# A hybrid decoder layer on one core: value stores of one pass on GpSimd's queue, the leading tokens' values in two passes with 48 stationary columns, and another order of the query stores and loads behind them

## The chip, the cores and the metric

The kernel runs on one core of a Trainium2 chip. The metric is the device time of one execution in microseconds (us); less is better. The kernel before takes 1297.9 us, the median of three runs (1297.64 to 1297.99).

A core has five engines that run side by side, each through its own list of instructions in order: TensorE (PE, matmuls; its weight loads are shown as PEld), VectorE (DVE), ScalarE (ACT), GpSimd (POOL) and SyncE (SP). They wait for each other on semaphores. Transfers between the chip's memory and the core's are issued by SP or by POOL in the order of their lists, and are carried out by 16 DMA engines.

## The reference

One layer: 16 learned leading ("meta") tokens are put before 1,024 tokens of 1,024 features. The normed input goes through one projection, whose columns feed two groups of heads. Four heads follow a gated delta rule (a triangular system per chunk of 64 tokens, then a scan over the chunks), eight heads of 64 columns make softmax attention with a cumulative forget gate in the logits. Their outputs are joined and projected, a SwiGLU feed-forward layer follows, then a last norm. The leading tokens are dropped at the end. All in float32.

```python
h = jnp.concatenate([meta, x], axis=1)
u = rmsnorm(h, attn_norm_w[l])
proj = u @ w_in[l]
gq, gk, gv, gz, gb, ga, fq, fk, fv, ff = jnp.split(proj, IN_SPLITS, axis=-1)
o_gdn = gated_deltanet_group(jnp.concatenate([gq, gk, gv], axis=-1), gz, gb, ga, ...)
o_fox = forgetting_attention_group(fq, fk, fv, ff, fgate_b[l])
h = h + jnp.concatenate([o_gdn, o_fox], axis=-1) @ w_out[l]
h = h + swiglu(rmsnorm(h, ffn_norm_w[l]), w_gate[l], w_up[l], w_down[l])
return rmsnorm(h, final_norm_w)[:, N_META:]
```

## The kernel before

Every matrix product is made of three matmuls, to come near float32: both operands are split into a high part (`uh`, `whi`) and a low part (`ul`, `wlo`), and high x high, low x high and high x low are added in PSUM (`mm3g`, line 214). The input `u` lies transposed in `uh` and `ul`, eight blocks of 128 features by 1,040 tokens, the 16 leading ones first. Tokens are handled in eight tiles of 128 (t = 0 to 7), and the leading tokens are a tile of their own, t = -1.

The program goes through these stages: the projections for the delta heads with their convolutions (up to about 190 us), the inversion of the triangular systems, the levels that join blocks of it and the scan over the chunks (up to about 420 us), attention with the first output projection between (up to about 590 us), the feed-forward layer, and the last norm.

During inversion, levels and scan, PE has little of its own to do there, so the attention's projections are woven in as filler. The generator `fox` makes them in this order: gates `z0`, values in two passes (`fv1`, 264 columns with the forget gate's eight, then `fv0`, 256 columns; `b` is 1, then 0), keys (`fk`) and queries (`fq`). The object `od` keeps account of how long each engine is busy, and takes from the filler whenever the steps of the levels and the scan are not yet due; `LV0` is the account at which the two runs of levels become due. The order that it finds is written into PE's list.

Per value tile, `proj_tmg` makes 24 matmuls (three for each of eight blocks) with the tokens as the stationary operand. ACT copies the high part from PSUM into `fvt`, DVE subtracts for the low part, and SP stores to `v_d`, or to `vz_d` for the leading tokens (four copies, one for each quarter that `vm` reads). The tiles run from t = -1 to t = 7. `ps_mm` rotates through three PSUM banks, and `fvt` has a few buffers in rotation.

The queries run in 12 groups, four blocks `m` of 128 rows by three stretches of tokens (from 16, 358 and 700). Each is 24 matmuls of 340 or 342 columns into a bank of `ps_mm`, then a copy by ACT and a subtraction by DVE into `fhl` (lines 777 and 778), which has two buffers in rotation, and a store to `q_d` (line 780), issued by POOL. Keys go the same way to `k_d`.

Attention takes the heads one after another. `att_tiles` sets up tiles for one head parity, with memsets of rows of `ka` and `qa` on POOL (lines 727 and 728); `att_head` issues the head's loads on SP: `ka` and `qa` from `c_d`, then `kk`, `sa`, `ka`, `qa` from `k_d` and `q_d`, `avt` from `v_d`, and with head 1 also `vm`, both tiles of it. PE then makes scores (`sc`), transposes (`pt`) and outputs (`po`). Between them stand the matmuls of the delta heads' output projection, `wog`, whose results are added to a tile `ht` loaded from `x` and stored to `h_d`.

`tc.issue_after` puts an instruction behind another one of the same queue in that queue's list; it adds no wait.

Of the kernel before, what the change touches and what calls it, by code (L numbers as in the profile page):

```python
# [32 lines left out]
LV0 = (72.0, 106.0)  # L33
# [64 lines left out]
def tile_hymba_layer(ctx, tc, x, meta, attn_norm_w, w_in, conv_w, a_log, dt_bias, gdn_norm_w,  # L98
# [213 lines left out]
    for t in range(NT):  # L312
        load_norm(t)
        if w is None:
            w = win_block(GZ + 256, 264, "z1")
            nc.sync.dma_start(gnw, gdn_norm_w.rearrange("o p -> p o"))
        acc = proj_tm(t, w, 0, 264, f"z1_{t}")
        nc.vector.tensor_copy(gt[:, t], acc[:, 256:264])
        zst = gate_out(t, acc, zp, "zt", 2)
# [4 lines left out]
    load_norm(-1)  # L324
    acc = proj_tm(-1, w, 256, 8, "zg")
# [269 lines left out]

    def b3(col):
        return col[:, :, None].broadcast_to([col.shape[0], col.shape[1], P])
# [108 lines left out]
    def proj_tmg(acc, t, w, n):  # L706
        col, rows = tok_cols(t)
        yield from mm3g(acc[:rows, :n], [(uh[:, k, col:col + rows], ul[:, k, col:col + rows], w[0][k][:, :n],
                                          w[1][k][:, :n]) for k in range(KT)], n / 2400)
# [52 lines left out]
    def fox_proj(dst, chunks, off, scale, nm):  # L762
        for b in range(2):
            w = fox_w.pop(0)
            for i in range(2):
                m = 2 * b + i
                for ci, (c0, n) in enumerate(chunks):
# [12 lines left out]
                    last[0] = nc.gpsimd.dma_start(dst(m)[:, :, c0 - off:c0 - off + n], hl[:, :, :n].bitcast(F32))  # L780
# [148 lines left out]
    def fox():  # L929
# [8 lines left out]
        for b in (1, 0):  # L938
            n = 256 + 8 * b
            w = fox_w.pop(0)  # L940
            for t in range(-1, NT):
                if t == (3 if b else 1):
                    fox_load()
# [3 lines left out]
                vt = fvp.tile([P, 4, 2, DH], F32R, tag="fvt", name=f"fvt{b}_{t}")  # L947
                av = acc[:rows, :256].rearrange("p (h d) -> p h d", d=DH)
                split(vt[:rows, :, 0], vt[:rows, :, 1], av)
                src = vt[:rows].rearrange("p h a d -> p h (a d)").bitcast(F32)  # L950
                if t < 0:
                    for j in range(GRP):
                        vst[0] = nc.sync.dma_start(
                            vz_d[4 * b:4 * b + 4, VZ * j:VZ * j + NM * 512].rearrange(
                                "h (r f) -> r h f", f=512)[:, :, 0:P], src)
                else:
                    vst[0] = nc.sync.dma_start(v_d[4 * b:4 * b + 4, col:col + rows].rearrange("h t d -> t h d"), src)
# [32 lines left out]
    att_tiles(1)  # L990
    hds[1] = att_head(1)
    while od.step_fill():
        pass
    uctx.close()
# [184 lines left out]
    def wout_gdn(nb, tt):  # L1179
# [9 lines left out]
        with tc.issue_after(h_st[-2].ins) if len(h_st) >= 2 else nullcontext():  # L1189
            nc.gpsimd.dma_start(ht, x[cols, nbc])  # L1190
# [556 lines left out]
```

## Time and profile before

| what | value |
| --- | --- |
| median of 3 runs | 1297.9 us (1297.64 to 1297.99) |
| the profiled execution, its own time | 1296.32 us |
| its span in the trace | 1294.6 us |
| granted clock of PE, mean | 0.998 |
| PE busy | 1277.3 us, 99% of the span |
| DVE, ACT, POOL busy | 840.4, 546.3, 367.9 us |
| DMA | 234.90 MB, 181 GB/s in the mean |

A row of the timeline gives the start in us from the span's start, the duration, the engine, the line and operation, out<-in, sizes, how many, and in square brackets the idle time of the engine before it and what ended that. PE's matmuls overlap one another by the way they are shown: their pace is the distance from start to start. A row of the chain of waits gives start, duration, and what the end of the program was waiting for then. A row of the list of waits gives the waiting engine, tile and line, what it waited for, the total in us, how often, and the longest. A row of the windows gives a stretch, its length, busy time (and the count of instructions) of the engines asked for, PE's granted clock, the busy share of the DMA engines, and GB/s. SPq and POOLq are issues of transfers.

### The profile page before, as it was taken

The numbers are of one execution on the slowest core, as the hardware profiler recorded it, in microseconds if no ns is written. First come the engines' busy times: TensorE is split into PE (matmuls) and PEld (weight loads), VectorE is DVE, ScalarE is ACT, GpSimd is POOL, SyncE is SP. The second block draws the span as 40 slices with busy tenths as digits, with TensorE's granted clock in tenths as the row PEclk, the third lists the DMA queues.
The fourth block names the chain that finished last, engine by engine and source line by source line (L and its number), as shares of the span: only waits on it lengthen the run. The fifth ranks groups of instructions, "written<-read, shape, count | busy, mean of one in ns | idle before, by whom it ended". The sixth has DMA issues, their size and how long they took to land.

```text
span 1294.6 us, 19961 instructions
## 1 busy us (share of the span) xinstructions
PE 1277.3 (99%) x7434; PEld 1126.3 (87%) x7434; DVE 840.4 (65%) x1508; ACT 546.3 (42%) x940; POOL 367.9 (28%) x342
## 2 busy tenths in 40 slices
PE   8999999999999999999999999999999999999998
PEld 8999999999999888887778888888888888888887
DVE  6567899574267488886887666655656664465645
ACT  6455444133234477884453323333333343433332
POOL 2012213102333212213405534455433453020301
PEclk9999999999999999999999999999999999999999
DMA  6433634677498778838434654553445468945513
GB/s 231 133 114 116 178 93 105 171 199 225 151 338 260 200 217 222 226 79 269 163 130 153 196 165 147 179 187 130 147 155 170 156 212 290 375 179 201 208 63 130
DMA packets 181840, 234.90 MB, mean 181 GB/s; under 512 B 19160, under 2 KB 132080, under 8 KB 178928
## 3 DMA queue, kind: packets, MB, share of 16 engines
q1 hardware_dynamic: 176048, 215.74, 52.0%
q0 software_dynamic: 5696, 17.90, 4.2%
q8 instruction: 58, 0.95, 0.3%
q14 instruction: 38, 0.31, 0.1%
HBM read 154.68 MB, written 78.92 MB: 180 GB/s over the span
## 4 chain that ended last, share of the span: by engine, by line
PE 89%; DMA 4%; DVE 3%; issue 2%; ACT 1%; POOL 1%; SPq 1%; POOLq 0%; DVEq 0%; ACTq 0%
PE xp L1628 9%; PE yp L1628 7%; PE ua L1453 5%; PE ga L1453 5%; PE gb L1453 5%; PE ud L1453 5%; PE gd L1453 5%; PE ub L1453 5%; PE pj_fk L214 4%; PE fv L214 3%; PE pt L1071 2%; PE ue L1453 2%; PE ge L1453 2%; PE wog L214 2%; PE z L214 2%
## 5 line engine op out<-in xcount | busy, mean ns | idle before, releaser
L166 DVE TENSOR_TENSOR al_p<-ra_p,ah_p 128x2048 fp32r<-128x2048 f32 (+1 forms) x21 | 46.6, 2221 | 93.9 <-ACT ah_p L165 93.9
L165 ACT CAST ah_p<-ra_p 128x2048 fp32r<-128x2048 f32 (+1 forms) x21 | 37.1, 1766 | 106.0 <-PE xp L1628 48.5
L1628 PE MATMUL xp<-wh_p,al_p 128*128 128x512 f32 (+1 forms) x176 | 67.3, 382 | 0.0
L1628 PE MATMUL xp<-wl_p,ah_p 128*128 128x512 f32 (+1 forms) x176 | 67.3, 382 | 0.0
L1628 PE MATMUL xp<-wh_p,ah_p 128*128 128x512 f32 (+1 forms) x176 | 67.3, 382 | 0.0
L1509 POOL TENSOR_TENSOR gzw<-gzw,uzt 128x512 f32<-128x512 f32 x11 | 18.4, 1676 | 164.9 <-DVE uzt L1498 113.6
L1453 PE MATMUL gb<-uh_p,w_g_p 128*128 128x512 f32 x176 | 57.8, 389 | 0.0
L1453 PE MATMUL ub<-uh_p,w_u_p 128*128 128x512 f32 x176 | 57.8, 389 | 0.0
L1453 PE MATMUL gd<-uh_p,w_g_p 128*128 128x512 f32 x176 | 57.8, 389 | 0.0
L1453 PE MATMUL ud<-uh_p,w_u_p 128*128 128x512 f32 x176 | 57.8, 389 | 0.0
L1509 POOL TENSOR_TENSOR gxy<-gxy,uxy 128x512 f32<-128x512 f32 x22 | 38.3, 1740 | 66.5 <-DVE uxy L1498 58.7
L166 DVE TENSOR_TENSOR w_u_p<-raw_u,w_u_p 128x512 fp32r<-128x512 f32 x42 | 43.2, 1027 | 20.3 <-ACT w_u_p L165 20.1
L165 ACT CAST ph<-pt 128x512 fp32r<-128x512 f32 (+1 forms) x96 | 45.4, 477 | 23.4 <-PE pt L1071 20.6
L166 DVE TENSOR_TENSOR pl<-pt,ph 128x512 fp32r<-128x512 f32 (+1 forms) x96 | 51.9, 553 | 4.5 <-ACT ph L165 4.0
L1035 ACT ACTIVATE pr<-pr,sm 128x144 f32<-128x144 f32 (+3 forms) x64 | 50.6, 793 | 6.0 <-DVE sm L1030 5.7
L1453 PE MATMUL ua<-uh_p,w_u_p 128*128 128x512 f32 x160 | 52.5, 389 | 0.0
L1453 PE MATMUL ga<-uh_p,w_g_p 128*128 128x512 f32 x160 | 52.5, 389 | 0.0
L1628 PE MATMUL yp<-wh_p,ah_p 128*128 128x512 f32 x132 | 51.3, 389 | 0.0
L1628 PE MATMUL yp<-wl_p,ah_p 128*128 128x512 f32 x132 | 51.3, 389 | 0.0
L1628 PE MATMUL yp<-wh_p,al_p 128*128 128x512 f32 x132 | 51.3, 389 | 0.0
L165 ACT CAST w_u_p<-raw_u 128x512 fp32r<-128x512 f32 x42 | 26.0, 620 | 55.3 <-PE gd L1453 35.6
L166 DVE TENSOR_TENSOR wl_p<-rw_p,wh_p 128x2048 fp32r<-128x2048 f32 (+1 forms) x21 | 46.9, 2235 | 3.4 <-ACT wh_p L165 3.4
(651 smaller groups left out, 4250.0 us busy)
## 6 DMA issues: line engine op xcount, KB each, us to landing
ra_p<-ao_p SPq DMA_DIRECT2D x14, 1024.0 KB
raw_g<-in_w_gate_dram SPq DMA_DIRECT2D x22, 512.0 KB
raw_u<-in_w_up_dram SPq DMA_DIRECT2D x22, 512.0 KB
raw_d<-in_w_down_dram SPq DMA_DIRECT2D x22, 512.0 KB
wt_p<-raw_d SPq DMA_DIRECT2D x33, 256.0 KB
rw_p<-wt_p SPq DMA_DIRECT2D x8, 1024.0 KB
rw_p<-in_w_down_dram SPq DMA_DIRECT2D x6, 1024.0 KB
ao_p<-gzw SPq DMA_DIRECT2D x22, 256.0 KB
```

The costliest lines, as they stand in the source:

```text
L165: cast = nc.scalar.copy(dst_hi, src)
L166: low = nc.vector.tensor_sub(dst_lo, src, dst_hi.bitcast(F32))
L214: nc.tensor.matmul(dst, a, b, start=first, stop=last)
L1035: nc.scalar.activation(pr[:, :n], pr[:, :n], AF.Exp, bias=sm[:, np_ - 1:np_], scale=-1.0, accum_out=rsum[:, h, j:j + 1])
L1071: nc.tensor.transpose(pt[:, P * j:P * j + P], pts[j][0][:, j, c0:c0 + P], ident)
L1453: nc.tensor.matmul(dst, a[:, c], b[:, k], start=(first and k == 0 and i == 0), stop=(k == 3 and i == 2), skip_group_check=not first)
L1509: last_mul[0] = G.tensor_tensor(gs[d], gs[d], us[d], op=ALU.mult)
L1628: nc.tensor.matmul(dst[:, n_], a[:, f, c], b[:, f, n_], start=(first and i == 0 and n == 0), stop=(i == NF - 1 and n == 2), skip_group_che ...
```

## The change

It has seven parts.

1. **Leading tokens' values in two passes.** A new tile `um_` holds, for each block of 128 features, the 16 leading tokens' high part in columns 0 to 15, zeros, and their low part in columns 32 to 47. With it as the stationary operand, one matmul with `whi` and one with `wlo` make all products, 16 matmuls for 24. The rows 32 to 47 of the result (the low part's) are copied out by ACT into a new buffer `vlo`, and DVE adds the rows 0 to 15 to it; then the tile goes on as before. (The product low x low is now included.) `um_` is zeroed by POOL and filled by ACT and DVE.
2. **Order of the value tiles.** The leading tokens come fourth, behind tiles 0, 1 and 2.
3. **Value stores of the pass b = 0** (eight to `v_d`, four to `vz_d`) are issued by POOL instead of SP. What was to be issued behind the last value store on SP (`vst`) now stands behind that of the pass b = 1.
4. **Key weights** are asked for at t = 2 in the pass b = 0, the third tile as before. The load of `gnw` is issued behind those of the normed input.
5. **Query stores.** Once the scan has made its last output (`outs_left` is empty), they are issued by SP: the last four of twelve. The first two loads of `ht` go on SP as well.
6. **Head 1's tiles and loads** stand behind the last query store on SP.
7. `LV0` is lower by 2, as the filler is shorter.

```diff
-LV0 = (72.0, 106.0)
+LV0 = (70.0, 104.0)
...
+    um_ = lp.tile([P, KT, 48], F32R, name="um_")
+    nc.gpsimd.memset(um_.bitcast(F32), 0.0)
+    nc.scalar.copy(um_[:, :, 0:NM], uh[:, :, 0:NM].bitcast(F32))
+    nc.vector.tensor_copy(um_[:, :, 32:48], ul[:, :, 0:NM].bitcast(F32))
...
     def proj_tmg(acc, t, w, n):
         col, rows = tok_cols(t)
+        if t < 0:
+            for k in range(KT):
+                for i in range(2):
+                    nc.tensor.matmul(acc[:48, :n], um_[:, k], w[i][k][:, :n], start=not (k or i), stop=k + i == KT)
+                    od.pe(n / 2400)
+                    yield
+            return
...
-                    last[0] = nc.gpsimd.dma_start(dst(m)[:, :, c0 - off:c0 - off + n], hl[:, :, :n].bitcast(F32))
+                    last[0] = (nc.gpsimd if outs_left else nc.sync).dma_start(dst(m)[:, :, c0 - off:c0 - off + n], hl[:, :, :n].bitcast(F32))
...
-            for t in range(-1, NT):
-                if t == (3 if b else 1):
+            for t in (0, 1, 2, -1, *range(3, NT)):
+                if t == (3 if b else 2):
                     fox_load()
                 col, rows = tok_cols(t)
                 acc = (ps_mm if b or t % 2 else ps_t)(f"fv{b}_{t}")
                 yield from proj_tmg(acc, t, w, n)
                 vt = fvp.tile([P, 4, 2, DH], F32R, tag="fvt", name=f"fvt{b}_{t}")
+                if t < 0:
+                    lo = fvp.tile([P, 4, 2, DH], F32, tag="fvt", name=f"vlo{b}").rearrange("p a b c -> p (a b c)")[:NM]
+                    nc.scalar.copy(lo[:, :n], acc[32:48, :n])
+                    nc.vector.tensor_add(lo[:, :n], acc[:NM, :n], lo[:, :n])
+                    acc = lo
...
-                        vst[0] = nc.sync.dma_start(
+                        st_ = (nc.sync if b else nc.gpsimd).dma_start(
...
-                    vst[0] = nc.sync.dma_start(v_d[4 * b:4 * b + 4, col:col + rows].rearrange("h t d -> t h d"), src)
+                    st_ = (nc.sync if b else nc.gpsimd).dma_start(
+                        v_d[4 * b:4 * b + 4, col:col + rows].rearrange("h t d -> t h d"), src)
+                if b:
+                    vst[0] = st_
...
-    att_tiles(1)
-    hds[1] = att_head(1)
+    with tc.issue_after(last[0].ins):
+        att_tiles(1)
     while od.step_fill():
         pass
+    with tc.issue_after(last[0].ins):
+        hds[1] = att_head(1)
...
-        with tc.issue_after(h_st[-2].ins) if len(h_st) >= 2 else nullcontext():
-            nc.gpsimd.dma_start(ht, x[cols, nbc])
+        early = len(h_st) < 2
+        with tc.issue_after((ra_ld[NT - 1] if early else h_st[-2]).ins):
+            (nc.sync if early else nc.gpsimd).dma_start(ht, x[cols, nbc])
```

Three places show what this does to the lists. The first is POOL's list at the end of the query projection, before. The names `fhl_fq_358`, `_700` and `_16` are the query groups by their first token, `zmask` is a mask for the attention.

```order
L220 TENSOR_TENSOR os_4794<-os_4794,mhalf 128x4
L727 MEMSET ka_4869 6x1040
L728 MEMSET qa_4870 6x1024
L1190 DMA ht_0_5005<-in_x_dram 128x512
L1190 DMA ht_0_5041<-in_x_dram 128x512
L780 DMA q_d<-fhl_fq_358_4826 128x2x342
L780 DMA q_d<-fhl_fq_700_4889 128x2x340
L780 DMA q_d<-fhl_fq_16_4918 128x2x342
L1013 MEMSET zmask 128x1040
L780 DMA q_d<-fhl_fq_358_4947 128x2x342
L1014 AFFINE_SELECT zmask<-zmask 128x128
L780 DMA q_d<-fhl_fq_700_4976 128x2x340
```

The same place on POOL with the change:

```order
L220 TENSOR_TENSOR os_4786<-os_4786,mhalf 128x4
L792 DMA q_d<-fhl_fq_358_4820 128x2x342
L739 MEMSET ka_4861 6x1040
L740 MEMSET qa_4862 6x1024
L1035 MEMSET zmask 128x1040
L1036 AFFINE_SELECT zmask<-zmask 128x128
L1217 DMA h_d<-ht_0_4999 128x512
```

Of five query stores one is left, ahead of the memsets; four stores and both loads of `ht` are gone from this list.

The second place is SP's list with the change, from head 0's last load into head 1's (`ka_4861`, `kk_4958` and the others are head 1's).

```order
L767 DMA avt_4707<-v_d 128x8x128
L1213 DMA ht_0_4999<-in_x_dram 128x512
L1213 DMA ht_0_5035<-in_x_dram 128x512
L792 DMA q_d<-fhl_fq_700_4867 128x2x340
L792 DMA q_d<-fhl_fq_16_4896 128x2x342
L792 DMA q_d<-fhl_fq_358_4925 128x2x342
L792 DMA q_d<-fhl_fq_700_4954 128x2x340
L758 DMA ka_4861<-c_d 3x1040
L759 DMA qa_4862<-c_d 3x1024
L762 DMA kk_4958<-k_d 64x1040
L763 DMA sa_4959<-q_d 64x1024
L762 DMA kk_4958<-k_d 64x1040
```

Before, head 1's eleven loads followed head 0's `avt` directly. Now two loads of `ht` and four query stores stand between.

The third place is PE's list in the first pass over the values. Before, the leading tokens' matmuls came first, with 16 stationary columns (the first size in a row), three for each block:

```order
L214 MATMUL z_7_2692<-whi_z_1_2480,ul 128x256
L214 MATMUL fv_-1_2720<-whi_fv_0_2514,uh 16x264
L214 MATMUL fv_-1_2720<-wlo_fv_0_2515,uh 16x264
L214 MATMUL fv_-1_2720<-whi_fv_0_2514,ul 16x264
L214 MATMUL fv_-1_2720<-whi_fv_0_2514,uh 16x264
```

With the change they follow the third tile, two for each block:

```order
L214 MATMUL fv_2_2784<-whi_fv_1_2524,uh 128x264
L214 MATMUL fv_2_2784<-wlo_fv_1_2525,uh 128x264
L214 MATMUL fv_2_2784<-whi_fv_1_2524,ul 128x264
L716 MATMUL fv_-1_2814<-whi_fv_0_2518,um__2467 48x264
L716 MATMUL fv_-1_2814<-wlo_fv_0_2519,um__2467 48x264
```

Over the program PE's list is shorter by 16 matmuls.

More of the change, by code (lines that the diff above doesn't have):

```diff
@@ L315, in tile_hymba_layer @@
             w = win_block(GZ + 256, 264, "z1")
-            nc.sync.dma_start(gnw, gdn_norm_w.rearrange("o p -> p o"))
         acc = proj_tm(t, w, 0, 264, f"z1_{t}")
@@ L324, in tile_hymba_layer @@
     load_norm(-1)
+    nc.sync.dma_start(gnw, gdn_norm_w.rearrange("o p -> p o"))
     acc = proj_tm(-1, w, 256, 8, "zg")
```

## The prediction

> **What bounds the kernel now.** The first view is the page's head: busy time of each engine as a share of the span, and the chain that ended last.
>
> ```profile
> span 1294.6 us, 19961 instructions
> PE 1277.3 (99%) x7434; PEld 1126.3 (87%) x7434; DVE 840.4 (65%) x1508; ACT 546.3 (42%) x940; POOL 367.9 (28%) x342
> PE 89%; DMA 4%; DVE 3%; issue 2%; ACT 1%; POOL 1%; SPq 1%; POOLq 0%; DVEq 0%; ACTq 0%
> ```
>
> TensorE (PE) is busy for 99% of the span and makes 89% of the chain. So a change can gain in two ways only: fewer matmuls, or an end to one of the few places where PE stands still or runs slowly. The second view says how much there is of the latter: PE's own waits, longest first.
>
> ```profile
> PE wog L214 <- DVE fhl_fq L778: 1.9, 1, 1.9
> PE sc L1025 <- DVE sm L1030: 1.7, 3, 0.6
> ```
>
> The longest single wait is one of 1.9 us, by the first output projection (`wog`), for VectorE's (DVE's) eviction of a query tile. The third view is PE's timeline around it, the fourth the chain there, the fifth the granted clock in slices of 2 us.
>
> ```profile
> 433.27 0.31 PE L214 MATMUL pj_fq<-uh,wlo_fq 128*128 128x340 f32 x1
> 435.48 0.58 PE L214 MATMUL wog<-whi_wo,uh_p 128*128 128x512 f32 x1 [1.89 <-DVE fhl_fq L778]
> ...
> 439.23 0.40 PE L214 MATMUL wog<-whi_wo,uh_p 128*128 128x512 f32 x1
> ...
> 439.93 0.23 PE L1025 MATMUL sc<-ka,qa 70*128 70x144 f32 x1
> ```
>
> ```profile
> 413.01 6.61 DMA qa<-q_d
> 419.62 0.95 POOL ka L727
> 420.58 0.89 POOL qa L728
> 421.47 2.63 issue
> 424.09 0.59 POOL ht L1190
> ...
> 425.32 8.99 DMA q_d<-fhl_fq
> 434.42 0.47 ACT fhl_fq L777
> 434.91 0.53 DVE fhl_fq L778
> 435.48 4.61 PE wog L214 x12
> ```
>
> ```profile
> 434.00:436.00 2.00, 0.53 (x2) 0.94 1.08 255
> 436.00:438.00 2.00, 2.00 (x7) 0.50 0.71 241
> 438.00:440.00 2.00, 2.00 (x9) 0.71 0.50 190
> ```
>
> Read the chain from below. `wog` needs a PSUM bank; the bank is freed by an eviction into a buffer `fhl`; that buffer is freed when its earlier content has been stored to `q_d`; and that store was issued late, because on GpSimd (POOL) two memsets and two loads of `ht` stood ahead of it, and the first memset waited for head 0's `qa`. PE loses twice. Matmuls of 340 columns follow each other every 0.155 us, so the next was due at 433.43; it started at 435.48: **2.05 us**. Then the granted clock falls to half (0.50 in the second of the three slices), and nine `wog` matmuls take 439.23 - 435.48 = 3.75 us. The three behind them take 439.93 - 439.23 = 0.70 us, or 0.233 each; nine at that pace are 2.10: **1.65 us** lost.
>
> **The change part by part.** *Fewer matmuls.* The chain has the two passes over the 16 leading tokens and what follows them:
>
> ```profile
> 232.81 2.91 PE fv_-1_2720 L214 x24
> ...
> 241.72 17.83 PE fv L214 x144
> 259.56 2.76 PE fv_-1_3005 L214 x24
> ```
>
> 24 matmuls become 16 in each pass, with as many moving columns (264 and 256). At 2.91/24 = 0.121 and 2.76/24 = 0.115 us each, 8 x 0.121 + 8 x 0.115 = **1.89 us**. The stationary operand grows from 16 columns to 48:
>
> ```profile
> L214 PEld LDWEIGHTS fv_-1_2720<-whi_fv,uh x8: 93/94/98, 232.5 to 235.1; 128*16 128x16 f32 x8
> ```
>
> ```profile
> L214 PEld LDWEIGHTS fv<-whi_fv,uh x128: 186/188/193, 235.4 to 284.3; 128*128 128x128 f32 x128
> ```
>
> The full tiles, with loads of 188 ns, keep the same pace (17.83/144 = 0.124, a stall among them), so 48 columns, between the two, cost nothing.
>
> *Building `um_`.* A memset on POOL, a copy on ScalarE (ACT), one on DVE. DVE's stands ahead of the whole second inversion (`up`), and the eviction that PE waits for at 241.72 stands behind six `up` operations:
>
> ```profile
> 239.78 0.16 POOL L546 MEMSET ad<- 128x32 f32 x1 [10.59 <-DMA ad<-ad_d]
> ...
> 239.97 0.16 DVE L533 TENSOR_TENSOR up<-up,ad 128x2 f32<-128x2 f32 x1 [13.26 <-DMA rec_d<-zt]
> ...
> 241.02 0.40 DVE L166 TENSOR_TENSOR fvt_-1_2745<-fv_-1_2720,fvt_-1_2745 16x256 fp32r<-16x256 f32 x1
> ```
>
> DVE sits idle for 13.26 us before 239.97. The memset needs the store of `e`, which the sync queue issued before the load of `ad`:
>
> ```profile
> 232.03 0.53 SPq L516 DMA_DIRECT2D rec_d<-e  x1
> 232.78 2.57 SPq L545 DMA_DIRECT2D ad<-ad_d  x2
> ```
>
> If the store lands with the second `ad` load, a memset of 0.4 us (POOL takes 0.53 for 128x512 in this stage, by the next row) and a copy like the 0.16 rows push PE's stall at 241.72 out by 0.6 us; if it lands 0.6 us sooner, nothing.
>
> ```profile
> 228.32 0.53 POOL L547 MEMSET up<- 128x512 f32 x1 [3.22 <-DMA ud_d<-up]
> ```
>
> It is issued some 2 us ahead of that second load, so I take **0**, and keep 0.6 for the range. PE itself reaches that bank after 72 matmuls as before, since three full tiles now stand where the leading tokens and two tiles stood.
>
> *The second copy and add for the leading tokens (ACT, DVE), and the `fr` copy from `vlo`*: two operations of 0.4 us per pass, beside at least 2.8 us of matmuls per tile, with three banks rotating. Nothing. *Value stores of the second pass on POOL*: in PE's list of waits no value eviction stands but the one at 241.72, so there is nothing to gain. What it could cost: POOL's memset of `amt`, which comes after DVE's last `up`, now stands behind three of these stores, the third of them behind DVE's eviction of the third tile:
>
> ```profile
> 270.08 0.42 DVE L166 TENSOR_TENSOR fvt<-fv,fvt 128x256 fp32r<-128x256 f32 x1
> 270.42 0.68 DVE L535 TENSOR_REDUCE up<-up 128x16 f32<-128x512 f32 x1
> ```
>
> The eviction ends 0.6 us before `up` does, so the store's issue delays the memset by well under 1 us, in a chain of small DVE operations that runs on beside PE's value tiles. Nothing either way; the key weights keep their place, at the third tile.
>
> *Query stores.* `q_d` 358 of the third block now goes ahead of POOL's memsets, and the last four stores go on the sync queue (SP), behind two early loads of `ht` but ahead of all of head 1's loads. Each waits only for its own eviction. The wait of 1.89 us has then no cause left. The bank needed at 433.4 is that of the group that ends 2 x 3.8 us (24 x 0.157 each) earlier, so a store may be 6 us late before PE feels it. I take off **2.05 + 1.65 = 3.70 us**.
>
> *Head 1's loads.* This is the price. They went out from 419.65; now they stand behind the last query store. PE's last query matmul ends at 433.58, now 433.58 - 1.89 = 431.69; ACT 0.47 and DVE 0.53 make it 432.7, and the store and the two short `c_d` loads put the first `kk` at about 434.1. Head 0's loads show the rest, six of them (two `kk`, two `sa`, `ka`, `qa`, 1,544 KB):
>
> ```profile
> 409.91 0.50 SPq L750 DMA_DIRECT2D kk<-k_d  x1
> ...
> 413.01 0.59 SPq L753 DMA_DIRECT2D qa<-q_d  x1
> ...
> 419.65 0.46 SPq L750 DMA_DIRECT2D kk<-k_d  x1
> ```
>
> `qa` landed at 413.01 + 6.61 = 419.62, 9.7 us after the first issue. So head 1's `qa` lands near 443.8. Its first score stood at 451.26 and moves to 451.26 - 5.59 = 445.7: 1.9 us in hand. But `avt` (512 KB) and the first `vm` (256 KB) follow, and `vm` is read 0.5 us later:
>
> ```profile
> 451.26 0.32 PE L1025 MATMUL sc<-ka,qa 70*128 70x144 f32 x1
> ...
> 451.80 0.56 PE L1092 MATMUL po<-phm,vm 128*128 128x128 f32 x4
> ```
>
> 768 KB more take 4.8 us at head 0's 1,544/9.7 = 159 KB/us, or 3.0 us at the rate of the stretch in which these loads ran before:
>
> ```profile
> 420.00:440.00 20.00, 18.11 (x103) 16.88 (x101) 5.12 (x9) 4.63 (x9) 6.85 (x10) 0.91 0.97 257
> ```
>
> `vm` lands at 446.8 to 448.6 and is wanted at 446.2: PE waits 0.6 to 2.4 us. I take **1.0**, nearer to the second rate, which is that of the same loads. A part may be caught up in the attention, so nothing is not excluded.
>
> **The sum**, against the profiled execution: -1.89 - 3.70 + 1.0 = -4.6 us, a span of 1290.0 for 1294.6, and 1291.7 for its own 1296.32 us. That execution is 1.6 us below the median of 1297.9; with the same difference the median becomes **1293.3 us**.
>
> One rule of the Trainium skill is weighed here ("TensorE: Matmul & The Clock Gate", section "What's actually happening"): the clock goes back to half after an idle window of about 3.4 us, and the window runs free. The length of the half-clock stretch agrees (windows 434 to 440: 0.06 x 2 + 0.50 x 2 + 0.29 x 2 = 1.7 us of lost clock, 3.4 us at half), the cause does not, since PE stood still for only 2.05 us before it. Taken by the letter, no idle time under 3.4 us halves the clock; the sum would then have no reason to take off the 1.65.
>
> **The rivals.** *A: head 1's loads come late and the clock falls too.* For it: a pause of 1.89 us was followed by the half-clock stretch above; waits of 0.6 us (second row of PE's waits) were not, so the point lies between. At 2.4 us of wait and 1.65 more, the gain is 5.59 - 4.05 = 1.5 us: 1296.4. Against it: it needs the slow end of the rates. *B: the change does not do what it says, PE still waits at `wog`.* On the sync queue the stores share the DMA engines with head 0's last loads (busy share 0.97 in that stretch); should one take the 9 us that the chain shows for it, the wait stays and only the matmuls are gained: 1296.0. Against it: there are 6 us to spare, and head 1's loads are out of the way. *C: the slow clock is not tied to the pause* and 3.4 us of it turn up wherever PE pauses next: only 1.89 + 2.05 - 1.0 = 2.9 us are gained, 1295.0. The sentences on the skill above would have it so; the trace has one such stretch, right behind its longest pause, which speaks against. *D: slower.* All of head 1's loads stand in one queue behind a store. If that last store, issued at 432.7, holds the sync queue or the DMA engines for the chain's 8.99 us, `kk` to `qa` land at 441.7 + 9.7 = 451.4 and `vm` 3.0 to 4.8 later, 454.4 to 456.2: a wait of 8.2 to 10 us in two or three pieces and one half-clock stretch, 1.65. Net 5.59 - 9.9 = 4.3 us lost: 1302.2. It passes the time of before from a wait of 4 us (with the 1.65), and slower by 0.2% from 6.6. Against it: an issue on that queue costs the queue some 0.6 us (row at 413.01), not the whole transfer.
>
> **How the numbers follow.** Forecast 0.62; A 0.15; B 0.09; C 0.06; D 0.08. 0.2%, 2.6 us, is about what a measurement of this kernel can tell from no change. Faster than 1295.3 are the forecast, C and a small part of A (0.02): 0.70. Within are the rest of A and B: 0.22. Slower: D, 0.08. The range begins at 1291.5: no wait at all (5.59 gained, 1292.3) and 0.8 more, half of what PE's second row of waits could still give where the order shifts. It ends at 1297.0, which takes in A and B with the 0.6 of `um_`. Outside it lie D and some 0.1 from the ends.
>
> **What would show it.** In the profile after: 16 matmuls fewer; `fv_-1` groups of 8 with 48 columns, near 1.9 us a pass; PE's wait at `wog` for `fhl_fq` gone; a granted clock of 1.00 in all slices after the start; the stall in front of the fourth value tile still 0.3 us, not 0.9. Head 1's `kk` issued near 434; a new wait `sc<-ka,qa` or `po<-phm,vm` near 446, of 0 to 2.4 us. Wrong would make it: a second half-clock stretch there (A), `q_d` stores that take 9 us (B), or a new place in the passes of the values or the levels where PE waits.

## The result, and the profile after

| kernel | median | range, runs | ratio to before [95%] |
| --- | --- | --- | --- |
| before | 1297.95 us | 1297.64 to 1298.7, 4 | 1 |
| after | 1305.12 us | 1303.97 to 1308.28, 4 | 1.0057 [1.0042, 1.0071] |

The change makes the kernel 7.2 us (0.57%) slower, where 4.6 us less was predicted and the range ended at 1297.0. The profiled execution of after is the slowest of its four (1308.28 us, span 1306.6).

The page's head, in the order of the prediction: span, busy time, chain by engine.

```profile
span 1306.6 us, 19944 instructions
PE 1280.3 (98%) x7418; PEld 1129.2 (86%) x7418; DVE 839.8 (64%) x1511; ACT 547.9 (42%) x943; POOL 370.8 (28%) x349
PE 81%; DVE 6%; DMA 5%; issue 3%; SPq 2%; ACT 1%; POOL 1%; POOLq 0%; DVEq 0%; ACTq 0%
```

PE makes 16 matmuls fewer, as planned, but its share of the chain falls from 89% to 81%: it waits more. PE's own waits:

```profile
PE sc L1047 <- DMA qa<-c_d: 4.1, 1, 4.1
PE pu L645 <- ACT y L638: 3.1, 2, 2.9
PE po L1114 <- DMA vm<-vz_d: 3.1, 1, 3.1
```

The wait of `wog` is gone, and three longer ones have come: one in the levels (`pu`), two at the start of head 1's attention. The granted clock in slices of 2 us at both places (length, PE busy, clock, DMA share, GB/s):

```profile
292.00:294.00 2.00, 0.16 (x2) 1.00 1.05 377
294.00:296.00 2.00, 0.69 (x16) 0.57 0.85 279
296.00:298.00 2.00, 2.00 (x58) 0.50 0.12 37
...
454.00:456.00 2.00, 0.00 (x0) 0.67 1.10 293
456.00:458.00 2.00, 1.21 (x3) 0.50 1.09 282
```

At both places the clock falls to half while PE waits. Where the time goes can be read by setting the starts of the same matmuls in the two traces side by side:

| matmul | before, us | after, us | after minus before |
| --- | --- | --- | --- |
| last of the values (`fv`) | 284.65 | 283.46 | -1.19 |
| last of the queries (`pj_fq`) | 433.27 | 438.21 | +4.94 |
| 13th of `wog` | 440.40 | 441.59 | +1.19 |
| last `pt` | 580.11 | 591.34 | +11.23 |
| last of all | 1288.14 | 1299.73 | +11.60 |

So there are two gains, 1.2 us up to the last value and 3.75 us at `wog`, where 1.89 and 3.70 were predicted. And there are two losses: 6.1 us between the values and the last query, and 10.0 us at the start of the attention.

**The loss in the levels.** The chain of after there (start, duration, what was waited for):

```profile
286.98 2.30 issue
...
289.30 4.41 DMA v_d<-fvt
...
293.78 0.37 ACT fvt L165
294.15 0.36 ACT fhl_fk L789
294.52 0.45 ACT y L638
...
295.62 1.91 PE pu L645 x62
```

`pu` needs `y`, a copy by ACT. In ACT's list the copy stands behind a cast of values into `fvt`. That cast waits for a store of an earlier `fvt` to land, and the store itself was held back on GpSimd's queue.

**The loss in the attention.** The chain of after from the last query matmul to head 1's first output:

```profile
435.90 2.49 PE pj_fq L214 x16
...
438.41 0.73 ACT whi_wo L168
...
439.17 0.65 DVE wlo_wo L169
...
440.54 0.51 DVE fhl_fq L790
...
441.06 0.36 SPq L792
...
442.27 0.47 SPq L762
...
447.17 3.91 SPq L748
...
451.13 9.85 DMA vm<-vz_d
...
461.11 1.09 PE po L1114 x4
```

The last query's eviction stands behind casts of the weights `wo` on ACT and DVE. Then come its store, head 1's loads from 442.27 (`kk` is the first large one), and the loads of `vm`: the first takes 3.91 us to be issued on SP (L748), the next, issued at 451.13, takes 9.85 us to land.

### The profile page after: what moved, and what is told of

It is laid out like the page before. It is cut to its first block, busy times and chain, and to the rows that moved or that the text cites. A ratio compares the mean times of both kernels' runs of the same rounds, so it can differ in the third digit from the quotient of the medians.

```text
span 1306.6 us, 19944 instructions
## 1 busy us (share of the span) xinstructions
PE 1280.3 (98%) x7418; PEld 1129.2 (86%) x7418; DVE 839.8 (64%) x1511; ACT 547.9 (42%) x943; POOL 370.8 (28%) x349
## 4 chain that ended last, share of the span: by engine, by line
PE 81%; DVE 6%; DMA 5%; issue 3%; SPq 2%; ACT 1%; POOL 1%; POOLq 0%; DVEq 0%; ACTq 0%
PE xp L1651 9%; PE yp L1651 7%; PE gd L1476 4%; PE ua L1476 4%; PE ga L1476 4%; PE gb L1476 4%; PE ud L1476 4%; PE ub L1476 4%; PE pj_fq L214 3%; PE pj_fk L214 3%; PE pt L1093 2%; PE ue L1476 2%; PE ge L1476 2%; PE po L1118 1%; PE wog L214 1%
```

## The experiments

Each run was measured in a batch with before. Before's medians in these batches lie between 1297.2 and 1297.74 us, so the ratio is what compares. Each diff is against the kernel that is named ahead of it.

### The attention: parts 5 and 6

**e2_h1_early**, after with head 1's tiles and loads where they were:

```diff
-    with tc.issue_after(last[0].ins):
-        att_tiles(1)
+    att_tiles(1)
+    hds[1] = att_head(1)
...
-    with tc.issue_after(last[0].ins):
-        hds[1] = att_head(1)
```

> The changed kernel with another part undone: head 1's tiles and loads are no longer tied to the last query store, and go out behind head 0's again. Theory 1 (head 1's loads come too late and cost two waits, 4.1 and 3.1 us, and slow clock on top, some 9 us): both waits at 450 to 462 us go, the time falls to about 1296; the four query stores on SP now stand behind head 1's loads, so a wait of up to 2 us at wog may come back (then 1299). Rival (the loads are late because DMA is slower with the stores on SP, whatever their order): the waits stay above 2 us each, the time above 1302.

Measured: 1302.97 us, 1.0039 [1.0025, 1.0054]. The waits for `qa` and `vm` are gone, so part 6 makes them. But a wait of 1.0 us at `wog` is back, and one of 3.4 us (`sc` for DVE's `sm`) is new: the query stores on SP now stand behind head 1's loads.

**e7_q_part**, before with parts 5 and 6 alone (their lines of the change's diff, nothing else).

> The kernel before with the query part of the change alone: four query stores and two loads of ht on SP, head 1's tiles and loads behind the last of these stores. Theory (this part gains 3.7 us at wog and loses more to late loads of head 1, by itself): no wait at wog, slow clock there gone, then waits for qa and vm of head 1 of 3 us or more each with slow clock behind them; 1297.2 - 3.7 + 9 = 1302. Rival (head 1's loads are late only because the levels were late and moved other transfers): waits under 2.4 us in all, the time 1294 to 1296.

Measured: 1303.21 us, 1.0041 [1.0026, 1.0056]. The 13th `wog` starts 3.54 us earlier than before, so the predicted 3.70 is there. Then PE waits (the scores read `ka` and `qa`; the list names `avt` as the one that came last):

```profile
PE po L1094 <- DMA vm<-vz_d: 3.8, 1, 3.8
PE sc L1027 <- DMA avt<-v_d: 3.5, 1, 3.5
```

The chain of this run shows the two steps that the prediction mis-sized:

```profile
433.68 0.74 ACT whi_wo L168
...
435.81 0.51 DVE fhl_fq L778
...
437.55 0.47 SPq L750
...
444.89 11.31 DMA vm<-vz_d
...
456.34 1.09 PE po L1094 x4
```

The first `kk` goes out at 437.55. The last query matmul starts at 433.48 here, so that is 4.1 us later; the prediction had 434.1 - 431.4 = 2.7. And `vm` lands at 456.20, 18.7 us behind the first `kk`, where 9.7 + 3.0 to 4.8 were predicted.

**e9_vm_early**, as e7, with the loads of both `vm` right behind head 0's loads:

```diff
+        vm_load(i)
...
-        if h:
-            for i in (0, 1) if h == 1 else (h,):
-                vm_load(i)
+        if h > 1:
+            vm_load(h)
```

> e7_q_part with one thing moved: the four loads of vm (512 KB), which need no query, stand right behind head 0's loads instead of last in head 1's. Theory (a load's landing is set by all that is in the queue with it, not by what stands ahead of it: 512 KB less in the burst behind the last query store lets every other load land some 2 us sooner, and vm itself is there): no wait for vm (3.8 us in e7_q_part), the wait for ka, qa and avt falls from 3.5 us to 1 to 2 us, the time from 1303.2 to about 1297. Rival (loads land in the order of the queue, the 9.7 us of head 0's loads hold, and the wait comes from the late start alone): the wait for qa stays at 3.5 us and only that for vm goes, 1299 to 1300.

Measured: 1297.28 us, 0.9994 [0.9985, 1.0003], 5.8 us less than e7 when each is set against its own before. The two waits are one now:

```profile
PE sc L1027 <- issue: 2.8, 1, 2.8
```

Most of the 5.8 us is `vm`'s own: its wait of 3.8 us is gone, and the half clock behind the waits lasts 6.8 us instead of 10.2. But `vm` had not only been late itself. With its 512 KB out of the burst, the loads ahead of it come down 0.7 us sooner: the wait of 3.5 us in front of `sc` becomes one of 2.8, less than the fall to 1 to 2 us that was expected. ("issue" says that the profile shows nothing that ended it.)

**e8_repair**, before with the memsets of head 1 on DVE and the first two loads of `ht` on SP behind head 1's loads. The cause of the wait at `wog` goes, and head 1's loads stay early:

```diff
-        nc.gpsimd.memset(ka[:NA].bitcast(F32), 1.0)
-        nc.gpsimd.memset(qa[:NA].bitcast(F32), -1.0)
+        ms = nc.vector if i else nc.gpsimd
+        ms.memset(ka[:NA].bitcast(F32), 1.0)
+        ms.memset(qa[:NA].bitcast(F32), -1.0)
...
-        with tc.issue_after(h_st[-2].ins) if len(h_st) >= 2 else nullcontext():
-            nc.gpsimd.dma_start(ht, x[cols, nbc])
+        early = len(h_st) < 2
+        with tc.issue_after((h_ld[1] if early else h_st[-2]).ins):
+            (nc.sync if early else nc.gpsimd).dma_start(ht, x[cols, nbc])
```

> The kernel before with another way to free GpSimd's queue for the query stores: they stay on GpSimd, but the two memsets of head 1's tiles go to VectorE and the two first loads of ht to SP behind head 1's loads, which stay where they were. Theory (the wait at wog came from what stood ahead of the stores, and head 1's early loads are free): no wait at wog, no slow clock at 436 to 439 us, no wait for head 1; 1297.2 - 3.7 = 1293.5 us. Rival (the stores are slow because of head 1's loads on the DMA engines): the wait at wog stays above 1 us and the time above 1296.

Measured: 1294.44 us, 0.9981 [0.997, 0.9991]. In the median the wait at `wog` can be had away for 3.3 us, if head 1's loads are not made to pay for it. The profiled execution, 1296.56 us, does not keep the gain: its 13th `wog` starts 3.35 us before that of before, but its last `pt` 0.06 us behind. One of head 0's scores (`sc`) waits 2.1 us for `sm`, and 3.4 us of half clock come with it. `sm` stands in DVE's list behind the addition to `ht`, and the load of `ht`, now behind head 1's loads, lands only at 438.74.

### The value stores: part 3

**e1_vstores_sp**, after with the value stores of both passes on SP:

```diff
-                        st_ = (nc.sync if b else nc.gpsimd).dma_start(
+                        st_ = nc.sync.dma_start(
...
-                    st_ = (nc.sync if b else nc.gpsimd).dma_start(
+                    st_ = nc.sync.dma_start(
```

> The changed kernel with one part undone: the value stores of the second pass go back from GpSimd's queue to SP's. Theory 1 (the stores on GpSimd go one at a time: each is issued about 0.3 us after the one before has landed, so the fvt buffers come free late, ScalarE stands before a cast, and its copy of y comes late for TensorE): the wait of 2.9 us for y in the levels and the slow clock behind it go, the order offset of TensorE at 300 us falls from +4.8 to about -1.5 us, and the time from 1305.1 to about 1299. Rival (ScalarE and VectorE are late because of the sync queue, whose key weights and na loads changed places, or because of um_): the wait stays at 2 us or more and the time stays within 2 us of 1305.

Measured: 1308.72 us, 1.0093 [1.0077, 1.0108]: slower than after. The stall only moves: PE waits 2.5 us at `pj_fk` for the `fvt` of DVE.

**e3_both**, e1 and e2 together.

> Both parts undone at once: value stores on SP, head 1's loads ahead of the last query stores. What is left of the change: 16 matmuls fewer, the order of the value tiles, four query stores and two loads of ht on SP. If the two costs are all there is and add up, 1305.1 - 6 - 9 = 1290 us; with a wait at wog come back, 1294. If they overlap (the second starts only because the first shifts things), 1296 or more.

Measured: 1304.57 us, 1.0053 [1.0038, 1.0068]. It is no faster than e2: putting both parts back gains nothing over putting head 1's loads back alone.

**e4_halves**, after with each value store on GpSimd's queue made as two halves of two heads:

```diff
-                    st_ = (nc.sync if b else nc.gpsimd).dma_start(
-                        v_d[4 * b:4 * b + 4, col:col + rows].rearrange("h t d -> t h d"), src)
+                    for h0 in (0,) if b else (0, 2):
+                        hn = 4 if b else 2
+                        st_ = (nc.sync if b else nc.gpsimd).dma_start(
+                            v_d[4 * b + h0:4 * b + h0 + hn, col:col + rows].rearrange("h t d -> t h d"), src[:, h0:h0 + hn])
```

> The changed kernel with each value store of the second pass on GpSimd's queue cut into two of two heads each, 256 rows of 512 bytes instead of 512. Theory 1 (GpSimd's queue holds a limited count of rows in flight, at least 768 and under 1,024): the two halves of a store go out back to back, and the first half of the next one too, without waiting for a landing; only the fourth half waits. The wait for y shrinks or goes. Rival (each store waits for the landing of the one before, whatever its size): every half is issued about 0.3 us after the half before has landed, the eight stores take longer in all than before and the wait for y grows.

Measured: 1304.61 us, 1.0056 [1.0036, 1.0076], two runs, as after. Its profile loses 2.7 us in the levels where after's loses 6.1, but the median doesn't follow. GpSimd's list in after shows why halves were tried:

```profile
289.30 0.76 POOL L974 DMA_DIRECT2D v_d<-fvt  x1 [2.32 <-issue]
294.01 0.76 POOL L974 DMA_DIRECT2D v_d<-fvt  x1 [3.96 <-issue]
```

The store issued at 289.30 lands at 293.71 (chain above), and the next goes out 0.30 us after that: on this queue the stores go one at a time.

**e5_vst**, e1 with `vst` set by every store again (part 3 undone in full), and **e6_own_vlo**, e5 with `vlo` in a buffer of `fhl` instead of `fvt`:

```diff
-                if b:
-                    vst[0] = st_
+                vst[0] = st_
...
-                    lo = fvp.tile([P, 4, 2, DH], F32, tag="fvt", name=f"vlo{b}").rearrange("p a b c -> p (a b c)")[:NM]
+                    lo = fp.tile([P, 2, 348], F32, tag="fhl", name=f"vlo{b}").rearrange("p a c -> p (a c)")[:NM]
```

> The changed kernel with its third part fully undone: the value stores of the second pass on SP as in e1_vstores_sp, and the loads for the levels (ubk, na) again behind the latest value store instead of the last one of the first pass, so the second level's 1 MB of na leaves the stretch from 265 to 282 us. Theory A (that load crowds the value stores out, whose landings free the fvt buffers): the value stores land in 5 us or less, TensorE's order offset at the end of the levels falls from +4.2 us to 0 or below, the time from 1308.7 to 1304. Rival B (vlo takes one of only three fvt buffers, and the leading tokens' stores come fourth): the offset stays at +3 us or more and the time within 2 us of 1308.7.

> As e5_vst, and vlo in a buffer of the pool of fhl, which is unused then, instead of in the rotation of three fvt buffers. Rival B of e5_vst: the waits of ScalarE for v_d stores between 260 and 290 us shrink, TensorE's waits at the first key matmuls go, and the offset at the end of the levels reaches about -1.5 us; time 3 us or more below e5_vst. If theory A was all: no difference to e5_vst beyond 1 us.

Measured: 1307.38 us, 1.0082 [1.0062, 1.0102], and 1308.69 us, 1.0085 [1.0065, 1.0105]. Both have a wait of 2.5 us at `pu` for `y`, as after has. So neither GpSimd's queue nor the rotation of `fvt` makes the loss in the levels by itself: between the last value and the last query e5 still loses 4.4 us and e6 4.5, where after loses 6.1. Without part 3 the kernel is 9.6 us slower than before (e5), with it 7.2: part 3 saves some 2.5 us, if anything (the intervals overlap; that of e1 is clear of after's).

### The values and the levels: parts 1, 2, 4 and 7

**e10_um_mixed**, before with `um_` (`vlo` in `fhl`), part 7, and the leading tokens fourth in the pass b = 1, first in b = 0. **e11_um_fourth** has them fourth in both and the key weights at t = 2: parts 1, 2, 4 and 7, but with `vlo` in `fhl` and the load of `gnw` where it was. **e13_best** is e10 with the edit of e8. From e10 to e11:

```diff
-            for t in (0, 1, 2, -1, *range(3, NT)) if b else range(-1, NT):
-                if t == (3 if b else 1):
+            for t in (0, 1, 2, -1, *range(3, NT)):
+                if t == (3 if b else 2):
```

> The kernel before with the 48-column values alone (um_, 16 matmuls fewer, vlo in a buffer of the fhl pool, LV0 lower by 2), value stores and the loads behind them as before; the leading tokens fourth in the first pass but first in the second. Theory (the stall in the levels comes from the fourth place in the second pass, which puts the four stores of the leading tokens into SP's list ahead of the second block of key weights, whose cast stands ahead of y on ScalarE): no wait of TensorE for y above 0.5 us, its order offset against before at 350 us is -1.2 to -1.6 us, the time 1296. Rival (um_ and the order of the first pass delay VectorE's inversion by themselves): offset above 0 at 350 us, the time 1298 or more.

> As e10_um_mixed, but the leading tokens fourth in both passes, as the change has it, and the key weights asked for at t = 2. Theory: the second block of key weights lands about 2 us later than in e10_um_mixed, TensorE waits some 2.5 us for y, the clock falls, offset at 350 us +2 to +3 us, the time about 1301. Rival of e10_um_mixed: no difference between the two beyond 1 us.

> e8_repair (memsets on VectorE, early ht on SP behind head 1's loads, query stores on GpSimd) together with e10_um_mixed (48 columns, leading tokens first in the second pass). If the two gains add: 1294.4 - 1.4 = 1293. If the 48 columns bring no gain by themselves: 1294 to 1296.

Measured: 1299.79 us, 1.0014 [1.0005, 1.0024]; 1300.94 us, 1.0021 [1.0012, 1.0031]; 1297.54 us, 0.9998 [0.9989, 1.0007]. The 48-column part alone does not gain 1.89 us but loses 2.1 to 3.3, although the last value matmul of e11 starts 1.15 us earlier than before's. The place of the leading tokens, with the key weights, makes 1.2 us of it in the medians, and the intervals overlap. Two causes were left: the second pass's value weights come late behind the leading tokens' stores (W), or part 7 (L).

**e15_lv0**, before with part 7 alone. **e14_um_lv0**, e11 without part 7:

```diff
-LV0 = (70.0, 104.0)
+LV0 = (72.0, 106.0)
```

> The kernel before with part 7 alone: LV0 of 70 and 104. The loads na and ubk of the first level then stand ahead of amt on the sync queue. Theory W: within 0.8 us of before, since the inversion is not touched. Theory L: 2 to 3 us slower, 1299.5 to 1300.5.

> The 48-column part alone, leading tokens fourth in both passes (as e11_um_fourth), with LV0 as before (72 and 106 instead of 70 and 104). Theory W (the second pass's value weights come late because their load stands behind the leading tokens' four stores; DVE's inversion stands behind the cast of these weights): LV0 does not matter, 1300.0 to 1301.5 as e11, and DVE's cast wlo_fv waits about 2 us again. Theory L (part 7, LV0 lower by 2, makes the first level's loads start too early and is what costs): near 1296.5, the inversion ends where it did before.

Measured: e15 1300.99 us, 1.0037 [1.0023, 1.0052]; e14 1293.84 us, 0.9976 [0.9967, 0.9985]. One number moves the 48-column part from 3.3 us lost to 3.45 gained, and alone it costs 3.7. L had the sign in both, and both by more than it expected. But not all of e14's gain is that of the saved matmuls. Set beside before, its trace is 0.84 us ahead at the last query and 4.58 us at the 13th `wog`: the wait there and its half clock are gone, which no edit of e14 aimed at, so that part is luck. 1.1 us are lost again later. The difference between e11 and e14 does arise at the levels: 6.9 of the 8.1 us between their profiled executions, from the last value to the last key matmul. How it works is read from the first matmuls of the levels (`py`: count, durations, first and last start) and what follows them. In e11:

```profile
L634 PE MATMUL py<-u,na x64: 191/191/212, 288.6 to 289.6; 32*32 32x32 f32 x64
```

```profile
291.84 1.04 ACT L165 CAST whi_fk<-raw_fk 128x1024 fp32r<-128x1024 f32 x1 [0.80 <-DMA raw_fk<-in_w_in_dram]
292.79 0.45 ACT L789 ACTIVATE fhl_fk<-pj_fk 128x348 fp32r<-128x348 f32 x1
293.14 1.16 ACT L638 COPY y<-py 32x512 f32<-32x512 f32 x2
```

```profile
PE pu L645 <- ACT y L638: 2.5, 2, 2.1
```

```profile
294.00:296.00 2.00, 1.65 (x63) 0.69 0.97 296
296.00:304.00 8.00, 8.00 (x42) 0.50 1.02 328
304.00:306.00 2.00, 2.00 (x15) 0.75 0.05 13
```

In e14, with `LV0` of before:

```profile
L634 PE MATMUL py<-u,na x64: 191/191/212, 290.4 to 291.4; 32*32 32x32 f32 x64
```

```profile
291.63 1.18 ACT L638 COPY y<-py 32x512 f32<-32x512 f32 x2 [0.21 <-PE py L634]
```

`LV0` says at which count of PE's work the levels are due. With 2 us less, the levels come due 1.8 us sooner (288.6 for 290.4; before 290.1). But `y` stands in ACT's list behind a cast of key weights, which hangs on their load, and these come no sooner: that cast starts at 291.84 in e11, at 290.01 in e14. So PE waits 2.1 us for `y`, and falls to half clock. The three rows give 0.31 x 2 + 0.50 x 8 + 0.25 x 2 = 5.1 us of lost clock; with the wait that is 7.2 us, which covers the 6.9. With `LV0` kept, the matmuls saved are made up with filler, `py` starts when it did before, PE does not wait at `pu`, and the clock stays at 1.00 from 288 to 306 us. In e15 `py` starts 2.0 us sooner than before, with new waits at `pu` in the levels (second row) and at head 0's scores (first row; 0.6 us was the longest there before):

```profile
PE sc L1025 <- DVE sm L1030: 4.1, 4, 2.5
PE pu L640 <- ACT y L633: 1.4, 2, 1.1
```

So e15 is not a clean price of the levels either. Its trace loses 2.2 us from the last value to the last query, wins 2.8 us at `wog`, where 0.6 us of wait is left, and loses 3.9 us from there to the last `pt`.

**e18_um_fifth**, e13 with the leading tokens fifth in b = 1, so that the value weights are asked for behind tile 2 as before. **e19_fifth_lv0**, the same with `LV0` of before.

```diff
-            for t in (0, 1, 2, -1, *range(3, NT)) if b else range(-1, NT):
+            for t in (0, 1, 2, 3, -1, *range(4, NT)) if b else range(-1, NT):
```

> As e13_best, with the leading tokens fifth instead of fourth in the pass b = 1, so that the second pass's value weights are asked for behind the store of tile 2 as before, and not behind the leading tokens' four stores. Theory W: raw_fv is asked for near 249.0 us instead of 250.7, the wait of 2.4 us at the first matmul of the second pass's leading tokens goes, and the time falls by 2 to 3 us to about 1295. Theory L: no difference to e13_best, 1297.0 to 1298.0.

> As e18_um_fifth with LV0 as before. Theory W: as e18, within 0.8 us. Theory L: 2 to 3 us faster than e18. Either way the candidate for a version better than both kernels: 1292.5 to 1295.

Measured: e18 1296.01 us, 0.9993 [0.9984, 1.0002], not to be told from e13. The wait of 2.4 us that W named has gone, but 1.3 us for `vlo` and 1.0 for `y` stand there instead. e19 1299.22 us, 1.0014 [1.0005, 1.0023]: 3.2 us slower than e18, which neither theory expected. Here keeping `LV0` costs, where from e11 to e14 it gained. Its profiled execution is the fastest of its eleven (1295.56 us), so its trace does not show where the others lose.

**e20_after_na**, after with the loads `na` of both levels moved behind the second inversion's stores to `ud_d`.

```diff
-                nc.sync.dma_start(ud_d[hp, b].rearrange("(j q) h t k -> q (h t) j k", q=2)[q], u3[r:r + 16])
+                ad_t["ud"] = nc.sync.dma_start(ud_d[hp, b].rearrange("(j q) h t k -> q (h t) j k", q=2)[q], u3[r:r + 16])
...
             nc.sync.dma_start(ubk, ud_d[hp].rearrange("b j h t k -> (b j) h t k"))
+        with tc.issue_after(ad_t["ud"].ins):
             for i in range(2):
                 nc.sync.dma_start(na[:, i], rec_d[:, :, 0, 2 * hp + i].rearrange("t p c -> p t c"))
```

> The changed kernel, with the loads na of both levels (2 MB) behind the second inversion's stores to ud_d on the sync queue, where the first level's stand in the kernel before; nothing else is undone. Theory N (the first level's loads, moved forward by part 7 and by part 3's narrower vst, fill the DMA engines while the value stores should land): the loss in the levels falls from 6 us to 2 or less, 1299 to 1301.5. Theory P (the value stores on GpSimd's queue go out one at a time, whatever else runs): the wait of PE at pu for y stays, 1304 to 1306.

Measured: 1308.25 us, 1.0081 [1.0067, 1.0094], slower than after. The wait at `pu` for `y` is gone, and this stands in its place:

```profile
PE py L635 <- DMA na<-rec_d: 3.8, 2, 2.7
```

So moving these loads, by whose place L had explained itself, does not win the time back, and P's wait did not stay either. Whether the loads are what makes `y` late where they stand early stays open. In the kernels with `LV0` of 70 that have a long wait there, it is not always for the same input: `fvt` in e1, `y` in e5 and e11, `na` here.

**e21_um_repair**, e14 with the edit of e8.

> The candidate: the 48-column part with LV0 as before (e14_um_lv0) and the repair of e8 (head 1's memsets on DVE, the first two loads of ht on the sync queue behind head 1's loads). If the two gains add (3.45 and 3.3 us), 1290.5 to 1291.5; if the wait at wog that e8 takes away has gone already in e14, as its list of waits says, no faster than e14, 1293.5 to 1294.5.

Measured: 1298.6 us, 1.0002 [0.9993, 1.0011]. Not as either expected: the two gains don't add, they cancel. The profile has its longest wait at head 0's scores:

```profile
PE sc L1043 <- DVE sm L1048: 4.9, 4, 3.2
```

e14 alone has no wait at `wog` any more, and 1.3 us as the longest of this kind. What the repair can take away is gone already, and the price that e8's trace showed is left. The chain of e21 has it:

```profile
432.62 7.73 DMA ht<-in_x_dram
...
440.45 0.06 DVE ht L1212
...
441.42 0.70 PE sc L1043
```

The load of `ht`, behind head 1's loads on SP, lands at 440.35. DVE's addition to `ht` waits for it, `sm` stands behind that on DVE, and the score behind `sm`; 6.8 us of half clock come with it. e19 has the same load and a wait of 2.7 us there. That is read from the traces; no run parts the loads of `ht` from the memsets. The best kernel found is thus e14 (1293.84) or e8 (1294.44), some 3.4 us below before.

## Why the prediction was wrong

Sorted by parts, in medians against each one's before: parts 1, 2 and 4 with `LV0` kept -3.45 (e14); part 7 on top of them +6.75 (e11 less e14); parts 5 and 6 +5.47 (e7). That makes +8.8. e5, which has all of these, measured +9.6, and e6, with `vlo` in `fhl` as e11 and e14 have it, +11.0. Part 3 then takes 2.5 off (after less e5, intervals overlapping): +7.2. The prediction had -1.89 for parts 1, 2, 4 and 7, and -2.7 for 5 and 6. The sum is a rough one: e14 and e7 both count the wait at `wog`, of which e11 still has 1.5 us.

- *Fewer matmuls, 1.89:* right in its mechanism; 1.19 us of it are there at the last value. The first group of 8 + 8 runs from 242.1 to 244.0 in after, near the 1.9 us a pass that was forecast, and 48 columns cost no pace. `um_` costs nothing: 0.38 us of stall in front of the fourth value tile.
- *The wait at `wog`, 2.05 + 1.65:* right. 3.54 us in e7, 3.75 in after.
- *Part 7:* the step that failed first is one that the prediction did not take. It gave `LV0` no line and so put it at nothing, as if shorter filler and an earlier due time were one thing. e15 measured +3.7 us for it alone, e11 less e14 +6.75 with the shorter filler: the levels come due 1.8 us sooner, `y` does not, and PE waits 2.1 us and runs at half clock. Against it stands one pair, e18 and e19, where the lower `LV0` is 3.2 us faster. In the changed kernel itself `LV0` was not put back, so its share of the 6.1 us there is argued, not shown; there e1, e5, e6 and e20 show that undoing the other parts at this place mostly changes what the levels wait for. A wait of PE in the levels was one of the prediction's own signs of being wrong.
- *"Value stores of the second pass on POOL ... Nothing either way":* the size was off, on the good side. The stores do go one at a time there, and they do set the end of the wait at `pu` in after's chain; but on SP the kernel is slower still (e1, e5).
- *Head 1's loads, +1.0 (0.6 to 2.4):* the mechanism was right, with the wait at the two places named, the size was not: 4.1 + 3.1 us of wait and the half clock behind them. Two steps of that sum failed. The last eviction was put straight behind the last query matmul, and stands behind the casts of `wo` (1.35 us, from 2.7 and 4.1); in the trace of before these casts already stand between the last evictions (DVE, 435.52 to 438.73). And the landing of `qa` and `vm` was worked out from what is issued ahead of them alone, at head 0's pace. In e7 avt, four `vm` loads, `ht` and the stores share the engines, and 18.7 us stand for 12.7 to 14.5. e9 bears on it: `vm` out of the burst gives back 5.8 us, though only 0.7 us of that is an earlier landing of what stood ahead of it. How the rest of the delay divides between `avt`, `ht`, the stores and the long issues on SP was not separated. (The six loads are 1,548 KB, not 1,544; nothing hangs on it.)
- *Rival D* had the sign, one of the two places and nearly the time (1302.2), but not the cause: no store holds the queue for its whole transfer. The last store takes 0.36 us to issue in after's chain (441.06), and the loads are late for the two reasons just named; what does hold SP there is an issue of head 1's own, the 3.91 us of `vm`. That the time is near is luck in part, since D had no loss in the levels. With the chance of 0.08 that it got, the range left it out.
- *Rival A* had waits of 2.4 us at most and half clock behind them; it failed on the same landing. *B* did not come: the wait at `wog` has gone. *C* did not come in after, where the half clock came with the two long pauses; in other runs the two do come apart (below).

What stays open: why `LV0` has the other sign between e18 and e19; and how the 6.1 us of after's levels divide between part 7 and the rest in that kernel, which after with `LV0` of before would have told.

## What to carry to other kernels

A due time in a planner's account of one engine is also a promise about the other engines: if that engine's work shrinks, the loads and casts that the steps need do not come sooner for it. So a change of a due time is a change of its own, to be priced and tried alone; here its sign differed from one pair of kernels to another. The landing of a load depends on what shares the burst with it, in part on what is issued behind it too; add up the bytes from the first issue to the landing, and not just those ahead. And edits that remove the same wait are tried together before they are added up.

## What was not expected of the hardware

**The clock does not go by the length of the pause alone.** In before a pause of 1.89 us was followed by half clock. In e19 PE waits 2.66 us before 439.71, and the clock stays at 1.00:

```profile
438.00:440.00 2.00, 0.29 (x1) 1.00 0.60 231
440.00:442.00 2.00, 2.00 (x13) 1.00 0.46 166
```

In e21 it falls with no pause at all. PE is busy throughout; 16 small matmuls (16x128) stand among the large ones between 352 and 355.5 us:

```profile
354.00:356.00 2.00, 2.00 (x13) 0.89 0.98 383
356.00:358.00 2.00, 2.00 (x10) 0.50 1.08 428
358.00:360.00 2.00, 2.00 (x13) 0.76 0.99 381
```

In e2 a pause of 1.03 us and one of 0.36 among small matmuls (32x32) are followed by some 10 us at half:

```profile
296.00:298.00 2.00, 1.58 (x6) 0.50 0.40 119
...
304.00:306.00 2.00, 2.00 (x21) 0.51 0.10 32
```

In all traces of this case the half-clock stretches between the start and the last 20 us are 3.4, 6.8 or 10.2 us long: one, two or three times the length of before's. The prediction's rival A put the point at which the clock falls between 0.6 and 1.9 us of pause; between 1.89 us with a fall and 2.66 us without, there is no such point. The Trainium skill ("TensorE: Matmul & The Clock Gate", section "What's actually happening") asks for an idle window of about 3.4 us; the length agrees, the idle time does not: in e21's case PE had not stood still, in e2's not for more than 1.03 us at a time, and in after the clock falls within the slice 294 to 296, some 2 us into a pause that begins at 292.2.

**GpSimd's queue carries fewer than two of these stores at a time.** In after no store of 128x4x128 goes out before the last of them has landed (281.02 and 281.33, 285.78 and 286.10, 293.71 and 294.01 for landing and next issue); in e4 three halves are in flight together and a fourth goes out 0.35 us behind a landing (287.44 and 287.79). On SP that order does not hold: in e11 seven other transfers are issued between such a store at 273.69 and its landing at 280.80. But the issue of that store takes 2.68 us by itself, so an issue on SP can be held up too.
